# A two-layer hybrid encoder on one core: third buffers for split weights, splitting two places ahead in output projections, phases of a layer that overlap, and new row maxima and key sums in attention

## The chip, the cores and the metric

The kernel runs on one core of one Trainium2 chip. The metric is the device time of one execution in microseconds (us). Five engines work side by side, each through its own list of instructions in order: TensorE (PE, matrix products and transposes), VectorE (DVE), ScalarE (ACT), GpSimd (POOL) and SyncE (SP, which here issues every DMA). An instruction that waits for another engine holds up everything behind it on its own engine.

## The reference

Two layers are applied to x (1024 tokens by 1024 features, float32). Each layer projects x with one wide matrix, feeds the columns to four mixers, and projects the four outputs back:

```python
h = jnp.einsum('bsd,dn->bsn', x, w_in[i])
y_a = attention_branch(...)   # 8 query heads, 2 key heads, axial rotary positions
y_h = hgrn2_branch(...)       # gated linear recurrence, forward and backward
y_s = ssd_branch(...)         # Mamba-2 form with a depthwise conv, forward and backward
y_g = gla_branch(...)         # gated linear attention, forward and backward
out = jnp.einsum('bsn,nd->bsd', concatenate([y_a, y_h, y_s, y_g]), w_out[i])
x = layer_norm(DEEPNORM_ALPHA * x + out, ln_g[i], ln_b[i])
```

Attention is a softmax over 1024 keys of 64 elements for each of 8 heads, multiplied by the values and by a gate.

## The kernel before, in words

Matrix products against weights are made exact enough by splitting: a weight tile of 128x1024 arrives by DMA in two halves (`wraw`), ACT rounds it to the fast float format (`whi`) and POOL subtracts to get the rest (`wlo`). The activations are split in the same way (`xh`, `xl`; for the output projection `mxh`, `mxl`). Each product is three passes: whi with xh, whi with xl, wlo with xh. `w_load` issues the two loads, `w_conv` makes the splits, `w_get` takes the pair for a place (one weight tile of one item), and `w_ahead` splits the next place and loads the one after. There are three buffers for raw halves and two each for `whi` and `wlo`.

The program is written by a planner at build time. Work of two kinds is queued. *Fill* items (`F(...)`) are the projections, which are long runs of matrix products: input projections into 1024 columns of PSUM (`proj`) or 512 (`projh`), and output projections (`oproj`). *Lane* items (`M(...)`) are the mixers, generators that yield what they wait for. At every step `run` takes the lane item that the plan's clock says is ready first, or a piece of fill: fill comes when no lane is ready within a slack of 100 ns, or when `plan.behind(share)` says that PE has streamed fewer columns than `share` of a threshold in the present window of 3413 ns. `KNOBS` holds the slack and the share (0.5). An item opens when the items that it names are done. The finished order is static.

One layer runs through these stages. The half projections of attention's inputs come first. Attention then works tile by tile of 128 queries: `a_qprep` norms, rotates and splits the queries (`qr`, `qhl`, transposed to `QT`); `a_s` multiplies QT by the high part of the keys into 1024 columns of PSUM (`S`) and takes the row maximum on DVE (`mx`), four times for each of two key heads; `a_e` computes the transposed scores (`ST`, twice per block: with QT and with `QM`, which carries the maxima), ACT exponentiates into `Pt`, and POOL adds the eight `Pt` blocks of a tile (`psum`) to give the softmax sums; `a_pv` multiplies by the values (`O`, 64 output rows) and takes the sums across keys (`Z`). Then come four HGRN heads (`hp`, `hn`, `hm`), the SSD branch (`sB`, `sC`, `sx` convolutions on DVE, `sm`, `sw`), and GLA in two pairs of heads (`gp`, `gn`, `gm`). HGRN and GLA share a tree of seven levels (`tree`, products `lv` of 32 or 64 columns, each level waiting for DVE), state products (`kst`, `P`) and outputs (`ot`); GLA adds a norm (`gss`) for each output. HGRN runs its tree on all 128 rows of the PE array, GLA on two halves of 64 rows. While GLA runs, only the 32 places of a layer's output projection are left as fill. `spec_proj` and `spec_post` compute the gates of GLA (`gk`, `ga`, `gm`) and the decays of SSD. The layer norm ends the layer (`lnT`, in the second layer `outT`).

SBUF is shared out in slots: 62 of 2 KB per partition (`k2`), 8 of 4 KB (`k4`), and others. The planner waits for a slot where none is free. Large results go through DRAM (`hdr`, `yd`).

All engine calls pass through the planner's wrapper, so nearly every row of the profile has the line of its call, 299 (300 in the changed kernel). Names such as `lv` or `wlo` tell the rows apart.

## Time and profile before

| | |
|---|---|
| median of 3 runs | 2640.66 us (2638.04 to 2647.71) |
| profiled execution, its own time | 2644.85 us |
| span of the profiled execution, first to last instruction | 2643.0 us |
| outside the span | 1.85 us |
| PE busy | 2481.6 us (94%) |
| DVE busy | 1588.1 us (60%) |
| ACT busy | 1092.9 us (41%) |
| POOL busy | 1227.7 us (46%) |
| mean granted PE clock | 0.970 |
| moved by DMA | 284.38 MB, mean 108 GB/s |

Busy time is the time in which at least one instruction of an engine runs. The granted clock is the share of full speed that the chip gave to PE; in this trace it is 1 or one half at any moment. A matrix product of 512 columns is shown with a duration near 400 ns, but they are pipelined: what counts is the time from one start to the next. A float32 product shows as two rows for one instruction in the program, a product in the fast format as one.

### The profile page before, as it was taken

Reading aid. Unit: us, or ns where it says so; the run is one execution under the profiler, and the core shown is the slowest. Engines: PE = TensorE matmul, PEld = TensorE weight load, DVE = VectorE, ACT = ScalarE, POOL = GpSimd, SP = SyncE. Lnnn points to the kernel's source line nnn. Section 1 sums busy time; section 2 is a strip of 40 time slices with the busy share of each in tenths; the row PEclk is TensorE's granted clock in tenths of the full one; section 3 lists DMA queues with packets and bytes.
Section 4 is the critical chain, followed back from the end, with each engine's and each line's share of the span. In section 5 each row is a group of like instructions: output and inputs, shape, how many; then the busy total and the mean of one; then the engine's idle time right before and its main releaser. Section 6 shows DMA issues by size and latency. Waiting matters only on the chain. (4 is left out here: it accounts for less than half of the span.)

```text
span 2643.0 us, 46508 instructions
## 1 busy us (share of the span) xinstructions
PE 2481.6 (94%) x18352; PEld 1855.2 (70%) x18352; DVE 1588.1 (60%) x2895; ACT 1092.9 (41%) x2100; POOL 1227.7 (46%) x932
## 2 busy tenths in 40 slices
PE   8999899999989997889989999999999999988996
PEld 6855457777877886667777655577777787866675
DVE  2574520565489778863555745206664898868737
ACT  4445453332464433334344444533334543433342
POOL 3556663223335446423554566642223454564334
PEclk9999999999989998989999999999999899999998
DMA  6311112011137447622343111120111365676232
GB/s 210 100 48 52 36 43 66 33 53 49 46 112 252 148 148 256 218 71 89 100 162 112 64 38 48 51 68 29 57 41 46 131 237 152 189 262 203 79 104 100
DMA packets 170173, 284.38 MB, mean 108 GB/s; under 512 B 17780, under 2 KB 43380, under 8 KB 169956
## 3 DMA queue, kind: packets, MB, share of 16 engines
q1 hardware_dynamic: 169956, 281.41, 32.5%
q8 instruction: 145, 2.38, 0.4%
q14 instruction: 72, 0.59, 0.1%
HBM read 205.39 MB, written 75.96 MB: 106 GB/s over the span
## 5 line engine op out<-in xcount | busy, mean ns | idle before, releaser
L299 POOL TENSOR_TENSOR wlo<-wraw,whi 128x512 fp32r<-128x512 f32 x372 | 509.9, 1391 | 585.3 <-ACT whi L299 528.7
L299 PE MATMUL proj<-xh,whi 128*128 128x512 f32 x1056 | 429.4, 407 | 4.7 <-DVE u L299 4.7
L299 PE MATMUL proj<-xl,whi 128*128 128x512 f32 x1056 | 415.1, 393 | 0.0
L299 PE MATMUL projh<-xh,whi 128*128 128x512 f32 x704 | 287.8, 409 | 10.4 <-ACT whi L299 9.6
L299 POOL TENSOR_TENSOR psum<-psum,Pt 128x1024 f32<-128x1024 f32 x96 | 228.6, 2381 | 128.2 <-ACT Pt L299 123.1
L299 ACT CAST whi<-wraw 128x512 fp32r<-128x512 f32 x372 | 216.6, 623 | 165.0 <-DMA wraw<-in_wt 63.7
L299 PE MATMUL proj<-xh,wlo 128*128 128x512 f32 x1056 | 281.0, 400 | 0.0
L299 PE MATMUL projh<-xl,whi 128*128 128x512 f32 x704 | 280.2, 398 | 0.3 <-DVE xl L299 0.3
L299 PEld LDWEIGHTS proj<-xh,whi 128*128 128x128 f32 x1056 | 199.6, 189 | 49.1 <-ACT ga L299 5.5
L299 PE MATMUL oproj<-mxh,whi 128*128 128x512 f32 x512 | 217.8, 425 | 15.9 <-ACT whi L299 9.2
L299 PEld LDWEIGHTS proj<-xl,whi 128*128 128x128 f32 x1056 | 200.2, 190 | 37.2
L299 PEld LDWEIGHTS proj<-xh,wlo 128*128 128x128 f32 x1056 | 192.6, 188 | 41.3 <-issue 2.1
L299 ACT ACTIVATE Pt<-ST 128x512 f32<-128x512 f32 x256 | 151.1, 597 | 135.6 <-PE ST L299 133.8
L299 PE MATMUL oproj<-mxl,whi 128*128 128x512 f32 x512 | 206.2, 403 | 0.0
L299 PE MATMUL projh<-xh,wlo 128*128 128x512 f32 x704 | 193.9, 398 | 0.0
L299 DVE TENSOR_REDUCE mx<-S 128x1 f32<-128x1024 f32 x128 | 151.9, 1218 | 53.5 <-PE S L299 52.4
L299 DVE TENSOR_TENSOR QP<-QP,T 128x512 f32<-128x512 f32 x168 | 144.7, 861 | 48.4 <-PE lv L299 47.5
L299 PEld LDWEIGHTS projh<-xh,whi 128*128 128x128 f32 x704 | 134.8, 192 | 54.9 <-issue 13.4
L299 ACT COPY M<-C 128x256 f32<-128x256 f32 x168 | 69.4, 415 | 241.2 <-DVE C L299 241.2
L299 PE MATMUL oproj<-mxh,wlo 128*128 128x512 f32 x512 | 152.7, 412 | 4.1 <-POOL wlo L299 4.1
L299 PEld LDWEIGHTS projh<-xl,whi 128*128 128x128 f32 x704 | 134.9, 192 | 27.5 <-DVE xl L299 1.5
L299 PEld LDWEIGHTS projh<-xh,wlo 128*128 128x128 f32 x704 | 129.0, 189 | 35.3 <-issue 9.7
(241 smaller groups left out, 4602.1 us busy)
## 6 DMA issues: line engine op xcount, KB each, us to landing
wraw<-in_wt SPq DMA_DIRECT2D x244, 256.0 KB
wraw<-in_wo SPq DMA_DIRECT2D x128, 256.0 KB
hdr<-zs SPq DMA_DIRECT2D x64, 256.0 KB
zs<-hdr SPq DMA_DIRECT2D x64, 256.0 KB
bc<-dr SPq DMA_DIRECT2D x64, 256.0 KB
yld<-yd SPq DMA_DIRECT2D x56, 256.0 KB
hdr<-sp SPq DMA_DIRECT2D x40, 256.0 KB
yd<-o SPq DMA_DIRECT2D x40, 256.0 KB
```

What stands on the lines that cost most here:

```text
L299: return real(*args, **kw)
```

## The change

**Buffers.** `whi` and `wlo` get three buffers each; the 2 KB slots go from 62 to 58. `w_ahead` also splits the second next place, and loads the third, when the next place belongs to another item or to an output projection.

**The planner.** The share in `KNOBS` goes from 0.5 to 1.0, and the cost of a POOL instruction from 155 + 2.09 n to 160 + 2.17 n.

**Row maxima.** The queries are also rounded whole (`qp`, ACT), transposed (`qpT`, PE) and copied (`Q2`, ACT). `a_s` multiplies two heads at a time, one on rows 0 to 63 of the array and one on rows 64 to 127, with half of the keys each time; DVE takes two maxima per instruction and then one maximum of two halves. The queries' low part is no longer in these maxima, which are only the shift of the softmax.

**Key sums.** The adds of the `Pt` blocks move from POOL to DVE.

**Phase borders.** `spec_proj` and `spec_post` come at the start of a layer instead of after HGRN's projections. The first HGRN projection opens after attention tile 4 instead of 6, and the HGRN mixers no longer wait for the last attention tile. From attention tile 4 on, at most 4 instead of 7 or 8 of the blocks `Pt` are live. SSD's groups and GLA's loads open earlier (after HGRN head 2, after SSD mixer 2, and so on). `a_pv` gets a lane of its own. The products `CB` of SSD are released earlier.

```diff
-NK2 = 62
+NK2 = 58
+H0, NQ = 4, 4
-KNOBS = ((None, 100, 0.5),)
+KNOBS = ((None, 100, 1.0),)
...
-                cost = 155 + 2.09 * n + (120 if fn == "tensor_copy" else 0)
+                cost = 160 + 2.17 * n + (120 if fn == "tensor_copy" else 0)
...
-    NB = {"k2": NK2, "k4": NK4, "wraw": 3, "whi": 2, "wlo": 2, "st": 24, "t2": 2, "t4": 2, "t8": 2, "ts32": 2, "ts16": 2, "ts8": 2, "ts4": 6,
+    NB = {"k2": NK2, "k4": NK4, "wraw": 3, "whi": 3, "wlo": 3, "st": 24, "t2": 2, "t4": 2, "t8": 2, "ts32": 2, "ts16": 2, "ts8": 2, "ts4": 6,
...
                 w_load(nk)
+                if nk[0] is not fcur[0] or nk[0].name.startswith("o"):
+                    w_conv(nk)
+                    nk = w_key(2)
+                    if nk is not None:
+                        w_load(nk)
...
             def second_half():
                 ins = h_in.pop(h)
+                yield ["k4:2"]
...
-            yield [spec, w2]
+            yield [spec, w2, "k2:12"]
...
+                    qp = k2("qp", F32R)
+                    ac.copy(qp, qr)
+                    yield [qp, "A:1"]
+                    pt = transpose4(lambda c: qp[:, ck(c)], "qpT", F32R)
+                    Q2 = k2("Q2", F32R)
+                    ac.copy(Q2, pt.bitcast(F32))
...
-                for c in range(4):
-                    yield [QT, "P:1"]
-                    S = bigps("S")
+                for c in range(2):
                     for sh in range(2):
-                        mm(hs(S, sh), QT[:, ck(c)], KK[g * 2][sh], True, True)
-                    yield [S]
-                    ve.tensor_reduce(out=mx[:, c:c + 1], in_=S, axis=AX.X, op=ALU.max)
-                    drop(S)
+                        yield [Q2, "P:1"]
+                        S = bigps("S")
+                        for e in range(2):
+                            r = slice(e * 64, e * 64 + 64)
+                            mm(hs(S, e), Q2[r, ck(2 * g + c)], KK[g * 2][sh][r], True, True)
+                        yield [S]
+                        ve.tensor_reduce(out=mx[:, sh * 4 + 2 * c:sh * 4 + 2 * c + 2], in_=AV(S, 0, [[HALF, 2], [1, HALF]]), axis=AX.X, op=ALU.max)
+                        drop(S)
+                tt(ve, mx[:, 0:4], mx[:, 0:4], mx[:, 4:8], ALU.max)
...
-                    yield [lambda: live[0] < NP[li], "k4:1"]
+                    yield [lambda: live[0] < (NP[li] if ti < H0 else NQ), "k4:1"]
...
-                        tt(gp, acc_s, pts[ti, 0], P, ALU.add)
+                        tt(ve, acc_s, pts[ti, 0], P, ALU.add)
...
-                        tt(gp, acc_s, acc_s, P, ALU.add)
+                        tt(ve, acc_s, acc_s, P, ALU.add)
...
+        F(f"sp{li}", spec_proj, after=x1 + [f"set{li}"], ws=[wsrc("sp")])
+        M(f"spp{li}", spec_post, needs=[f"sp{li}"], lane=3)
-            M(f"aP{li}{ti}", a_pv(ti), needs=[f"akv{li}a", f"akv{li}b", f"az{li}3"])
+            M(f"aP{li}{ti}", a_pv(ti), needs=[f"akv{li}a", f"akv{li}b", f"az{li}3"], lane=11)
-            F(f"hp{li}{h}", h_proj(h), after=[f"hm{li}{h - 2}"] if h > 1 else [f"set{li}", f"aP{li}6" if h == 0 else f"aP{li}7"],
+            F(f"hp{li}{h}", h_proj(h), after=[f"hm{li}{h - 2}"] if h > 1 else [f"set{li}", f"aP{li}{H0}" if h == 0 else f"aP{li}7"],
-            M(f"hn{li}{h}", a, needs=[f"hp{li}{h}", f"aP{li}7"])
+            M(f"hn{li}{h}", a, needs=[f"hp{li}{h}"])
-        F(f"sp{li}", spec_proj, after=[f"hp{li}3"], ws=[wsrc("sp")])
-        M(f"spp{li}", spec_post, needs=[f"sp{li}", f"hm{li}2"], lane=3)
-            M(f"sgp{li}{g}", s_group_post(g), needs=[f"sB{li}{g}", f"sC{li}{g}"] + (exps if g == 0 else [f"sm{li}0"]), lane=3)
+            M(f"sgp{li}{g}", s_group_post(g), needs=[f"sB{li}{g}", f"sC{li}{g}"] + ([f"hm{li}2"] if g == 0 else [f"sw{li}1"]), lane=3)
-            M(f"gp{li}{p}", g_load(p), needs=names + ([f"sm{li}3"] if p == 0 else [f"gn{li}0"]), lane=8)
+            M(f"gp{li}{p}", g_load(p), needs=names + ([xlast, f"sm{li}2"] if p == 0 else [f"sm{li}3"]), lane=8)
```

How the order of instructions moves is shown at three places.

**VectorE in attention, first layer.** Before, the rows are the row maxima (`mx<-S`), what is made of them (`qhl`), a tile's result (`ya`) and a gate of the fill (`zs`):

```order
L299 TENSOR_REDUCE mx<-S 128x1 x4
L299 TENSOR_SCALAR qhl<-mx 128x4
L299 SCALAR_TENSOR_TENSOR qhl<-mx,qhl 128x4
L299 TENSOR_REDUCE mx<-S 128x1 x3
L299 TENSOR_TENSOR ya<-O,rz 128x512
L299 TENSOR_REDUCE mx<-S 128x1
```

In the changed kernel, the same engine and stage:

```order
L300 TENSOR_REDUCE mx<-S 128x2
L300 TENSOR_TENSOR psum<-psum,Pt 128x1024
L300 TENSOR_REDUCE mx<-S 128x2 x2
L300 TENSOR_TENSOR mx<-mx 128x4
L300 TENSOR_SCALAR qhl<-mx 128x4
L300 SCALAR_TENSOR_TENSOR qhl<-mx,qhl 128x4
L300 TENSOR_TENSOR psum<-psum,Pt 128x1024
```

The adds of `Pt` now stand between the maxima; POOL's list, which had 112 of them, has none left.

**TensorE in GLA, first layer, second pair of heads.** `lv ... 64x64` are the last two levels of the tree, `oproj` is the fill. Before:

```order
L299 MATMUL lv<-QP,M 64x64 x16
L299 MATMUL oproj<-mxh,whi 128x512
L299 MATMUL oproj<-mxl,whi 128x512
L299 MATMUL lv<-QP,M 64x64 x16
L299 MATMUL oproj<-mxh,whi 128x512
```

In the changed kernel:

```order
L300 MATMUL lv<-QP,M 64x64 x16
L300 MATMUL oproj<-mxh,whi 128x512
L300 MATMUL oproj<-mxl,whi 128x512
L300 MATMUL oproj<-mxh,whi 128x512
L300 MATMUL oproj<-mxl,whi 128x512
L300 MATMUL oproj<-mxh,whi 128x512
L300 MATMUL oproj<-mxl,whi 128x512
L300 MATMUL oproj<-mxh,wlo 128x512 x4
L300 MATMUL oproj<-mxh,whi 128x512
L300 MATMUL oproj<-mxl,whi 128x512
L300 MATMUL lv<-QP,M 64x64 x16
```

Between these two levels stood 2 products of fill, and now 12. Counted over the order from GLA's first `lv` to its last `gss`, a layer has 324 output-projection products inside GLA in the first layer and 392 in the second before, 502 and 472 after; behind it stand 358 and 242 before, 202 and 176 after.

**SyncE at the first output projection, first layer.** `yld` are the mixer results that it reads, `wraw<-in_wo` its weights, `M`, `q` and `T` GLA's inputs. Before:

```order
L299 DMA hdr<-u 128x512
L299 DMA yld<-yd 128x512 x4
L299 DMA wraw<-in_wo 128x512 x4
L299 DMA xr<-in_xT 128x512
L299 DMA hdr<-zs 128x512 x2
```

In the changed kernel:

```order
L300 DMA yld<-yd 128x512 x4
L300 DMA M<-hdr 128x512
L300 DMA q<-hdr 128x512
L300 DMA T_9150<-hdr 128x512 x2
L300 DMA wraw<-in_wo 128x512 x4
L300 DMA hdr<-zs 128x512
```

Four loads of GLA now stand between the results and the first output weights.

More of the change, by code (lines that the diff above doesn't have):

```diff
@@ L1265, in gen @@
                     yield None
-                sd["g", g] = (Cc, CB, Bt)
+                sd["g", g] = (Cc, Bt)
+                sd["cb", g] = CB
             return gen
@@ L1290, in gen @@
                 colA, dr = sd["colA"], sd["dr"]
-                CB = sd["g", n // 2][1]
+                CB = sd["cb", n // 2] if n % 2 == 0 else sd.pop(("cb", n // 2))
                 def rows(hf, e):
@@ L1592, in gen @@
                         ac.copy(QT, pt.bitcast(F32))
-                        qts[ti, g] = (QT, qhl)
+                        qts[ti, g] = (QT, Q2, qhl)
             return gen
@@ L1600, in gen @@
                 yield [lambda: (ti, g) in qts]
-                QT, qhl = qts.pop((ti, g))
-                mx = mt("c8", [128, 4], name="mx")
-                for c in range(4):
-                    yield [QT, "P:1"]
-                    S = bigps("S")
-                    for sh in range(2):
-                        mm(hs(S, sh), QT[:, ck(c)], KK[g * 2][sh], True, True)
-                    yield [S]
-                    ve.tensor_reduce(out=mx[:, c:c + 1], in_=S, axis=AX.X, op=ALU.max)
-                    drop(S)
+                QT, Q2, qhl = qts.pop((ti, g))
+                mx = mt("c8", [128, 8], name="mx")
+                for c in range(2):
+                    for sh in range(2):
+                        yield [Q2, "P:1"]
[6 more added lines that the diff above has]
+                        drop(S)
+                del Q2
+                tt(ve, mx[:, 0:4], mx[:, 0:4], mx[:, 4:8], ALU.max)
+                mx = mx[:, 0:4]
                 mh = AV(qhl, 64, [[128, 4]])
```

4 lines of the change are left out of this document (2 added, 2 removed).

## The prediction, written before the changed kernel ran

> **What bounds the kernel now.** I read the page's first part, then PE's time by stages, PE's waits, and single groups and instructions.
>
> The page's first part:
>
> ```profile
> PE 2481.6 (94%) x18352; PEld 1855.2 (70%) x18352; DVE 1588.1 (60%) x2895; ACT 1092.9 (41%) x2100; POOL 1227.7 (46%) x932
> ```
>
> PE is the bound over the whole program, with 2643.0 - 2481.6 = 161 us in which it does nothing. To that comes time at half clock: a mean clock of 0.970 is a loss of 0.03 x 2643 = 79 us if PE had work all that time. So at most some 240 us can be won without taking work off PE. The windows by stage tell where they lie. The columns are the stretch, then its length, and for PE, PEld, DVE, ACT and POOL the busy time, then granted clock, DMA share and GB/s:
>
> ```profile
> 154.00:396.00 242.00, 222.36 (x927) 126.42 (x928) 117.86 (x131) 121.32 (x201) 150.91 (x77) 0.98 0.13 41
> 396.00:726.00 330.00, 327.39 (x3045) 253.37 (x3042) 147.25 (x316) 115.95 (x232) 104.02 (x91) 1.00 0.15 50
> 726.00:770.00 44.00, 37.34 (x298) 27.46 (x297) 37.04 (x52) 30.67 (x48) 20.21 (x18) 0.84 0.27 97
> 990.00:1041.00 51.00, 37.17 (x193) 30.55 (x192) 40.12 (x76) 18.12 (x36) 32.59 (x26) 0.87 0.81 254
> 1041.00:1197.00 156.00, 135.12 (x2263) 99.06 (x2261) 117.40 (x229) 53.37 (x103) 66.16 (x66) 0.88 0.45 150
> 1320.00:1408.00 88.00, 76.86 (x335) 61.69 (x334) 46.37 (x82) 39.82 (x71) 47.95 (x38) 0.94 0.49 164
> 1496.00:1628.00 132.00, 122.90 (x517) 71.73 (x517) 70.95 (x87) 67.25 (x112) 81.60 (x43) 0.96 0.15 48
> 2046.00:2068.00 22.00, 17.46 (x171) 10.46 (x169) 20.71 (x31) 15.62 (x24) 6.49 (x5) 0.73 0.29 108
> 2310.00:2360.00 50.00, 43.20 (x212) 33.88 (x210) 33.34 (x52) 17.91 (x32) 35.66 (x28) 0.93 0.78 251
> 2360.00:2553.00 193.00, 174.49 (x2508) 129.16 (x2508) 133.35 (x258) 68.85 (x130) 76.91 (x77) 0.96 0.44 147
> 2618.00:2643.00 25.00, 1.96 (x14) 1.35 (x12) 18.59 (x34) 3.84 (x14) 7.45 (x5) 0.59 0.30 115
> ```
>
> I call a stage's *loss* its idle PE time plus (1 - clock) times its length. HGRN's stretch (396 to 726) loses 3 us: there nothing is to be won. GLA loses 20.9 + 18.7 = 39.6 us in the first layer (1041 to 1197) and 18.5 + 7.7 = 26.2 in the second (2360 to 2553). The end of HGRN, where the gates are computed, loses 13.7 and 10.5 (726 to 770, 2046 to 2068). The entry to the output projections loses 20.4 and 10.3, with the DMA engines at 0.81 and 0.78. Attention loses 24.4 and 14.4. The layer border (1320 to 1408) and the last 25 us are not touched by the change. PE's waits name what ends them:
>
> ```profile
> PE lv L299 <- DVE QP L299: 12.8, 26, 1.6
> PE projh L299 <- ACT whi L299: 9.6, 4, 5.5
> PE oproj L299 <- ACT whi L299: 9.2, 1, 9.2
> PE gk L299 <- DVE near L299: 4.8, 2, 3.0
> PE proj L299 <- DVE u L299: 4.7, 2, 2.8
> PE oproj L299 <- POOL wlo L299: 4.1, 5, 2.3
> ```
>
> No single wait is large: the loss is many short ones (us in total, times, longest), and the half clock after them.
>
> **The change, part by part.** *Products of the row maxima.* The old pair of S, the start of a group of four transposes, and two stretches of `ot`, which HGRN does on all 128 rows and GLA in turn on 128 (AT) and 64 rows (QP). First the S pair (start, duration):
>
> ```profile
> 200.26 0.46 PE L299 MATMUL qmT<-ident,qhl 128*128 128x128 f32 x4
> 200.55 0.69 PE L299 MATMUL projh<-xh,wlo 128*128 128x512 f32 x2
> ...
> 204.75 0.62 PE L299 MATMUL S<-KK,QT 128*128 128x512 f32 x2
> 205.20 0.39 PE L299 MATMUL ST<-QT,KK 128*128 128x512 f32 x1
> 205.43 0.39 PE L299 MATMUL ST<-QM,KK 128*128 128x512 f32 x1
> ```
>
> Then HGRN's `ot`, and GLA's:
>
> ```profile
> 1989.51 0.39 PE L299 MATMUL ot<-AT,V 128*128 128x128 f32 x2
> 1989.73 0.61 PE L299 MATMUL ot<-QP,S 128*128 128x128 f32 x4
> 1990.18 0.39 PE L299 MATMUL ot<-AT,V 128*128 128x128 f32 x2
> ```
>
> ```profile
> 2449.30 0.49 PE L299 MATMUL ot<-AT,V 128*128 128x128 f32 x2
> 2449.72 0.71 PE L299 MATMUL ot<-QP,S 64*128 64x128 f32 x4
> 2450.36 0.49 PE L299 MATMUL ot<-AT,V 128*128 128x128 f32 x2
> ```
>
> A pair of S takes 205.20 - 204.75 = 0.45 us, a product 0.23. The same six `ot` take 0.67 us in HGRN and 1.06 in GLA: going to half the rows and back costs 0.39 us. The change has 128 pairs of S on half the rows, in the order almost always between products on all rows. If the halves run at once, a pair takes 0.23 + 0.39 = 0.62, or 0.17 more than now: +22 us. If they run one after the other, 0.84: +50. If the halves run at once and the turn costs nothing, -0.22 each: -28. I take +22, since the turn is in the trace. The new transposes are 16 groups of four at 0.29: +5. Together +27 us of PE work in a stage that is bound by PE.
>
> The Trainium skill speaks for the other end: TensorEngine Tiling (Array Packing), section Theoretical Speedup, gives up to twice the speed where the contraction is 64 or less, and the sum by that alone would be the -28 for this part. Its section Key Properties says that changing the tiling mode drains the engine; the 0.39 us agrees with that.
>
> *Key sums.* The rows for what moves, and for what VectorE takes for such operands:
>
> ```profile
> L299 POOL TENSOR_TENSOR psum<-psum,Pt 128x1024 f32<-128x1024 f32 x96 | 228.6, 2381 | 128.2 <-ACT Pt L299 123.1 <-PE S L299 4.4
> L299 POOL TENSOR_TENSOR psum<-Pt 128x1024 f32<-128x1024 f32 x16 | 38.0, 2377 | 23.5 <-ACT Pt L299 23.5
> L299 DVE TENSOR_TENSOR QP<-q,T 128x1024 f32<-128x1024 f32 x24 | 34.6, 1443 | 7.5 <-DMA T<-hdr 7.5
> L299 DVE TENSOR_TENSOR QP<-QP,T 128x512 f32<-128x512 f32 x168 | 144.7, 861 | 48.4 <-PE lv L299 47.5
> L299 DVE TENSOR_TENSOR acc<-acc,oproj 128x512 f32<-128x512 f32 x96 | 62.5, 680 | 64.3 <-PE oproj L299 63.7
> ```
>
> POOL is rid of 267 us. DVE has no such add now: twice 680 to twice 861 ns are the ends, 1.36 to 1.72 us, and the 1443 of a row with the same size and two operands in SBUF is nearest. 56 adds a layer are 81 us. DVE's load in two equal stretches of attention:
>
> ```profile
> 132.00:396.00 264.00, 244.36 (x1024) 140.18 (x1024) 135.44 (x152) 129.53 (x216) 162.51 (x82) 0.98 0.14 44
> 1452.00:1716.00 264.00, 253.67 (x1101) 155.13 (x1102) 137.30 (x165) 132.39 (x224) 167.42 (x85) 0.98 0.15 48
> ```
>
> 137 + 81 = 218 of 264 us, or 83%. PE's fill hides it while DVE keeps up, so I cost it at nothing; that cover is the first rival below. The other additions (two ACT copies per tile, a maximum of 4 columns on DVE) go the same way; ACT stands at half there (130 of 264).
>
> *Attention's losses*, 24.4 + 14.4 = 39 us: what is won is bounded by 0 and 39. POOL's splits no longer queue behind 2.38 us adds, and HGRN's projections come in as fill; DVE gets slower to answer. I take 11.
>
> *Fill beside GLA.* The order puts 178 more output products beside GLA in the first layer and 80 in the second; at 0.23 us these are 41 and 18 us of work that now stands alone. They can hide at most the stage's loss, 39.6 and 26.2, and at most their own length: so the ends are 0 and 39.6 + 18 = 58. I take about 70%, 28 and 12, because the order is fixed in advance and some gaps fall elsewhere.
>
> *Gates early.* `gk` and its chain leave the end of HGRN, where the losses are 13.7 + 10.5 = 24 us. The convolutions (`u`), which DVE does there, stay. Ends 0 and 24; I take 14, since the wait of `gk` (4.8) is as long as that for `u` (4.7) and the half clock follows both. In attention, where they go, the gates find a PE that has fill.
>
> *Third buffers and two places ahead.* They can take the waits for `wlo` (4.1) and part of those for `whi` in `projh` (9.6, of which one of 5.5): ends 0 and 14, I take 5. The wait of 9.2 us for the first output weights stays, since raw halves still have three buffers and the first item's loads come late. In the changed order four more loads of 128x512 float32 stand before them on SyncE: 4 x 0.262 MB at the 254 GB/s of that stage are 4 us later. What queues behind them is the first `whi`, and PE behind that. Net 1 us won. The four slots fewer are made up by `CB` being released early; if not, loads of GLA wait, inside the bounds above.
>
> *The sum.* Won: 28 + 12 + 14 + 1 + 11 = 66. Added: 27. Net -39 on the profiled execution's 2644.85 us: 2605.9. That execution is 4.2 us above the median of 2640.66, so the forecast is 2601.7, written as 2602 us.
>
> **The rivals.** *VectorE becomes the bound of attention.* Adds stand between the maxima that PE waits for, and S has only two buffers. With the gates' VectorE work, which I put at some 6 us a layer from this row, DVE has 224 of 264 us to do:
>
> ```profile
> L299 DVE TENSOR_SCALAR gm<-gk,pk 128x512 f32<-128x512 f32 x16 | 11.6, 748 | 6.2 <-ACT ga L299 5.9
> ```
>
> It decides once DVE's remaining idle is over 264 - 224 = 40 us a stage. It idles 127 now; if half of that stays, the stage needs 288: 24 us more a layer, 48 in all, and the 11 us are not won. 2602 + 48 + 11 = 2661, slower than before. For it speaks DVE's 83%; against it, that attention gets more fill, which PE can do while DVE is late. Chance 0.16.
>
> *GLA is bound by its own chain.* Each of its levels waits for DVE (`lv` on `QP`), and DVE is busy 117 of 156 us. Then more fill beside it makes the stage longer by as much as is taken off behind it, but for half: 20 of the 40 are not won, and attention wins nothing (11). 2602 + 31 = 2633, no change. That the splits two places ahead do little, as raw halves remain three, is included. Chance 0.17.
>
> *The halves of S run at once and turn for free.* Then the part gives -28 instead of +22: 2602 - 50 = 2552. Against it stands the 0.39 us of `ot`; for it, that `ot`'s halves depend on each other's sums and those of S do not. Chance 0.12. This is what the Trainium skill's speedup of up to two (TensorEngine Tiling, Theoretical Speedup) would give.
>
> **How the numbers follow.** The forecast has 0.55, with its own range of 2575 to 2627 from the ends of its terms taken a third of the way. The range reaches from just below the third rival to the first: 2545 to 2661. About 0.5%, 13 us, is what a measurement of this kernel can tell from no change: faster means below 2627.5, slower above 2653.9. Faster: 0.52 of the forecast, 0.12, and 0.07 of the second rival: 0.71. Slower: 0.14 of the first rival and 0.01 of the second: 0.15. The rest, 0.14, is the same.
>
> **What would show it.** In the changed profile, S should appear with 64 rows, and the time from the start of a pair to the next product should be near 0.6 us; 0.25 or less would prove the third rival. GLA's two stretches should have a clock near 1 and losses of some 12 and 14 us in place of 39.6 and 26.2. `gk` should lie inside attention, and the end of HGRN lose some 5 us each time. DVE should be busy 80 to 90% in attention with PE still over 92%; PE below that, waiting for `qhl` or for S's buffers, would prove the first rival. PE's busy time should rise, not fall, by about what S adds, and its idle time drop by some 40 us. The prediction is wrong if attention plus HGRN take longer than before by more than 30 us, or if GLA's stretches lose as much as now.

## The result, and the profile after

The changed kernel takes 2705.49 us (median of 4 runs, 2700.67 to 2707.48), the kernel before 2641.24 us beside it: a ratio of 1.0237, with a 95% interval of 1.0213 to 1.0262. It is some 63 us slower, where 39 us less were forecast, and it lies outside the range. Ratios compare fast executions alone: one execution of the run with the maxima alone took 5380.06 us at a clock of 0.459, and its ratio leaves that one out. The profiled execution took 2700.67 us, with a span of 2698.9 us against 2643.0: 55.9 us more.

TensorE's busy time on the first part of the page after, beside the other engines:

```profile
PE 2506.7 (93%) x18416; PEld 1837.8 (68%) x18416; DVE 1676.4 (62%) x3039; ACT 1111.9 (41%) x2134; POOL 955.4 (35%) x820
```

TensorE is idle for 2698.9 - 2506.7 = 192 us instead of 161, and its mean clock is 0.968 instead of 0.970. In the prediction's count (idle + (1 - clock) x length) the loss is 279 us instead of 240, 39 more; by this count the other 17 us of the 56 are work. The forecast had a loss 66 us smaller and 27 us more work.

Where the loss lies is read from windows by stage. The borders are events, so that they fit both kernels: attention from its first key transpose to its last `Z`, the middle (HGRN, SSD) from there to the first `oproj`, the output stage (the end of SSD, GLA, output products) from there to the first `lnT`, or to the last product in the second layer. Before, first and then second layer:

```profile
57.00:415.00 358.00, 334.89 (x1447) 206.80 (x1447) 177.09 (x261) 168.35 (x321) 210.41 (x123) 0.99 0.18 58
415.00:1008.00 593.00, 569.86 (x4500) 459.20 (x4496) 381.25 (x745) 236.48 (x455) 220.55 (x186) 0.98 0.33 107
1008.00:1277.00 269.00, 243.16 (x2779) 184.84 (x2780) 169.06 (x308) 95.63 (x177) 125.61 (x112) 0.92 0.45 149
...
1390.00:1739.00 349.00, 335.99 (x1481) 215.24 (x1483) 170.21 (x263) 170.81 (x325) 213.93 (x125) 0.99 0.19 62
1739.00:2315.00 576.00, 564.39 (x4477) 453.69 (x4474) 391.10 (x757) 232.84 (x449) 219.31 (x187) 0.99 0.33 108
2315.00:2620.00 305.00, 279.35 (x2999) 212.44 (x2999) 200.68 (x372) 114.18 (x250) 144.90 (x127) 0.96 0.46 151
```

The same stages of the changed kernel:

```profile
57.00:466.00 409.00, 393.19 (x1697) 239.63 (x1699) 229.05 (x335) 189.61 (x360) 97.61 (x79) 0.98 0.18 59
466.00:1010.00 544.00, 518.98 (x4262) 417.37 (x4262) 351.48 (x722) 224.67 (x428) 191.66 (x171) 0.98 0.34 110
1010.00:1290.00 280.00, 239.73 (x2806) 182.25 (x2806) 180.38 (x327) 97.63 (x184) 133.80 (x117) 0.93 0.45 145
...
1400.00:1812.00 412.00, 383.54 (x1662) 226.09 (x1662) 253.04 (x368) 219.33 (x402) 102.97 (x85) 0.99 0.20 64
1812.00:2338.00 526.00, 520.00 (x4248) 420.05 (x4249) 326.02 (x651) 185.08 (x371) 179.99 (x161) 1.00 0.32 102
2338.00:2676.00 338.00, 302.71 (x3083) 232.30 (x3082) 239.49 (x445) 121.75 (x267) 158.68 (x137) 0.91 0.46 148
```

Each row's length less PE's busy time, plus half of its time at half clock (taken from the trace's clock record, finer than the two decimals shown), gives the losses:

| loss in us | before | after | forecast of the change | measured |
|---|---|---|---|---|
| attention, both layers | 28.2 + 18.1 | 22.6 + 31.9 | -11 | +8 |
| middle, both layers | 35.0 + 18.4 | 35.2 + 7.7 | -14 | -11 |
| output stage, both layers | 48.1 + 37.6 | 59.1 + 66.0 | -41 (28 + 12 + 1) | +39 |
| layer border | 14.9 | 16.9 | 0 | +2 |

The output stages lose where they should have won, and this is 80 of the 95 us by which the forecast was wrong. TensorE's waits name what ends them (us in total, times, longest):

```profile
PE oproj L300 <- DVE acc L300: 30.2, 11, 7.5
PE projh L300 <- ACT whi L300: 17.9, 6, 5.7
PE oproj L300 <- ACT whi L300: 14.2, 2, 9.7
...
PE qpT L300 <- ACT Pt L300: 8.6, 4, 4.1
```

Output products wait 30.2 us for `acc`, 5.3 before. That is VectorE adding `xr` to a product's result, and it frees the PSUM buffer for the next product. Why it comes late stands in SyncE's own list (start, duration) at the first output products of the changed kernel:

```profile
1019.67 8.41 SPq L300 DMA_DIRECT2D wraw<-in_wo  x4
...
1028.61 0.42 SPq L300 DMA_DIRECT2D xr<-in_xT  x1
```

Four raw halves are issued in a row against three buffers. SyncE stands 8.41 us in them, and the load of `xr` that VectorE needs is behind.

In the second layer the last products of GLA are alone. The windows of that stretch (the columns as before):

```profile
2576.80:2587.00 10.20, 8.17 (x44) 6.07 (x45) 3.08 (x10) 1.70 (x4) 2.58 (x8) 0.50 0.33 96
2587.00:2597.00 10.00, 8.61 (x25) 5.71 (x25) 0.46 (x1) 2.62 (x4) 0.00 (x0) 0.50 0.03 10
2597.00:2607.00 10.00, 7.72 (x22) 4.99 (x22) 0.57 (x2) 2.94 (x5) 1.27 (x1) 0.50 0.00 0
2607.00:2614.00 7.00, 6.79 (x30) 5.34 (x30) 4.88 (x8) 2.33 (x5) 1.27 (x1) 0.50 0.00 0
```

For 44.4 us from 2576.8 on the clock is one half, which costs 22 us of work at full speed.

Finally, SSD now runs beside GLA: its last run of products `yo` begins 51 us (first layer) and 54 us (second) after GLA's first `lv`, where it began 11 and 20 us ahead of it before. "SSD's end" below means this start. The first layer, before and then after (start, duration):

```profile
1030.63 1.83 PE L299 MATMUL yo<-u,S 128*128 128x128 f32 x14
...
1041.51 0.76 PE L299 MATMUL lv<-q,ks 64*32 64x32 f32 x64
```

```profile
1040.00 0.76 PE L300 MATMUL lv<-q,ks 64*32 64x32 f32 x64
...
1090.93 1.83 PE L300 MATMUL yo<-u,S 128*128 128x128 f32 x14
```

### The profile page after: what moved, and what is told of

Its sections match the earlier page's. It is cut to its first block, busy times and chain, and to the rows that moved or that the text cites. A ratio compares the mean times of both kernels' runs of the same rounds, so it can differ in the third digit from the quotient of the medians.

```text
span 2698.9 us, 46777 instructions
## 1 busy us (share of the span) xinstructions
PE 2506.7 (93%) x18416; PEld 1837.8 (68%) x18416; DVE 1676.4 (62%) x3039; ACT 1111.9 (41%) x2134; POOL 955.4 (35%) x820
## 5 line engine op out<-in xcount | busy, mean ns | idle before, releaser
L300 PE MATMUL projh<-xh,whi 128*128 128x512 f32 x704 | 293.2, 416 | 21.4 <-ACT whi L300 17.9
L300 PE MATMUL oproj<-mxh,whi 128*128 128x512 f32 x512 | 220.9, 432 | 45.6 <-DVE acc L300 30.2
L300 PEld LDWEIGHTS proj<-xh,whi 128*128 128x128 f32 x1056 | 199.0, 188 | 55.9 <-issue 7.9
L300 PEld LDWEIGHTS proj<-xh,wlo 128*128 128x128 f32 x1056 | 193.7, 189 | 41.5 <-issue 1.7
L300 DVE TENSOR_TENSOR QP<-QP,T 128x512 f32<-128x512 f32 x168 | 157.6, 938 | 43.3 <-PE lv L300 42.4
L300 DVE TENSOR_TENSOR psum<-psum,Pt 128x1024 f32<-128x1024 f32 x96 | 121.1, 1262 | 100.5 <-ACT Pt L300 99.9
L300 DVE TENSOR_REDUCE mx<-S 128x2 f32<-128x1024 f32 x128 | 154.2, 1219 | 36.1 <-PE S L300 35.9
L300 PEld LDWEIGHTS oproj<-mxh,whi 128*128 128x128 f32 x512 | 100.8, 197 | 74.7 <-ACT whi L300 18.2
```

The source lines that it names most:

```text
L300: return real(*args, **kw)
```

## The experiments

Ratios are to runs of the kernel before on the same chip, with 95% intervals; 0.01 is 26 us. The expectations count a stage's loss a little differently: its length less its products at the median time from one start to the next in the first two traces. That gives larger numbers (67 and 77 for the output stages after) in the same order. My theory at the outset had three costs: SyncE's stops, fill spent too early beside GLA, and S on half rows; the rivals stand in each expectation. The runs are grouped by question, not by time. The planner lays out everything that follows an edit anew, so four runs were built to keep the order of the changed kernel, or of another run, on the engines that compute.

### SyncE's stops: the third load later, all else in the same order

The second argument makes `w_load` hold its two loads back until the next weight is asked for, behind `xr`. Only SyncE's list differs from the changed kernel's. Of the edit, the call:

```diff
-                        w_load(nk)
+                        w_load(nk, nk[0].name.startswith("o"))
```

> The changed kernel with the same order on TensorE, VectorE, ScalarE and GpSimd. Only on SyncE the two loads of the third place's raw halves, where they are for an output projection, stand later: behind the next load of xr, or before the next weight is taken. Nothing is left out. My theory: these loads wait for raw buffers and hold up xr behind them, so SyncE's stops of 7 to 8 us shrink to about half, TensorE's wait of output products for acc falls from 30 us to some 15, and the time by 10 to 20 us: about 2690 us. Rival: SyncE is held up by the second place's loads already, or acc waits for VectorE's own queue: the same time within 5 us. Rival two: the weights come later and TensorE waits for whi instead: slower by 5 to 10 us.

Measured: 2689.99 us, ratio 1.0210 (1.0182 to 1.0237); the span is 11.8 us shorter than after. SyncE at the same place, and TensorE's wait:

```profile
1020.19 1.04 SPq L300 DMA_DIRECT2D wraw<-in_wo  x2
1021.42 0.33 SPq L300 DMA_DIRECT2D hdr<-u  x1
1022.11 0.33 SPq L300 DMA_DIRECT2D xr<-in_xT  x1
...
1023.50 5.43 SPq L322 DMA_DIRECT2D wraw<-in_wo  x2
```

```profile
PE oproj L300 <- DVE acc L300: 16.6, 6, 5.8
PE oproj L300 <- ACT whi L300: 14.7, 2, 10.3
```

`xr` is issued 6.5 us earlier, the wait for `acc` falls from 30.2 to 16.6, and that for `whi` does not grow. The two output stages lose 16 us less (59.1 + 66.0 to 55.2 + 53.9). The stops are a cause. Their size is less sure here: 12 us by the spans, 15.5 by the medians, and 7 by the ratios, whose intervals overlap (1.0213 to 1.0262 for the changed kernel).

### One place ahead again

```diff
-                if nk[0] is not fcur[0] or nk[0].name.startswith("o"):
-                    w_conv(nk)
-                    nk = w_key(2)
-                    if nk is not None:
-                        w_load(nk)
```

> The changed kernel with the five lines taken out that split two places ahead; third buffers for split weights stay, and nothing of the computation is left out. The planner orders the rest anew, so some 10 us of scatter are to be allowed for. My theory: with three raw halves, splitting two places ahead makes SyncE wait inside the weight loads, and the loads of xr behind them come late; VectorE's adds of xr and then TensorE wait. Then TensorE's wait of output products for acc goes from 30 us to below 10, SyncE's long weight loads (7 to 8 us) go, and the time is 15 to 30 us shorter: about 2680 us. Rival: the splits two places ahead are what the third buffers are for, and without them TensorE waits for whi and wlo: the waits for whi grow by what those for acc lose, the time stays at 2700 to 2710 us or grows.

Measured: 2689.52 us, 1.0191 (1.0174 to 1.0208). The time is as I expected, but the wait for `acc` fell only to 17.8 us, and the waits for `whi` of output products grew from 14.2 to 16.9: part of each theory. The loss fell by 20 us in the second layer's output stage (66.0 to 45.5), but rose by 4 in the first layer's, and it fell by 14 in the first layer's attention (22.6 to 8.5), where no output products are; so this run shows a new order as much as its edit.

### GLA after SSD

```diff
-            M(f"gp{li}{p}", g_load(p), needs=names + ([xlast, f"sm{li}2"] if p == 0 else [f"sm{li}3"]), lane=8)
+            M(f"gp{li}{p}", g_load(p), needs=names + ([f"sm{li}3"] if p == 0 else [f"gn{li}0"]), lane=8)
```

> The changed kernel with GLA's loads opening as before (first pair of heads after SSD's last mixer, second pair after the first has begun); nothing is left out, and the planner orders what follows anew. In the kernel before with the borders alone, GLA ran beside SSD for 13 us in the first layer, where the output stage lost 6 us less than before, and for 51 us in the second, where it lost 28 us more. Theory: two chains of mixers beside each other wait on VectorE and GpSimd and use up the fill, so without the overlap the two output stages lose 60 + 55 us instead of 67 + 77, and the time is 15 to 30 us shorter: about 2683 us. Rival: the overlap is harmless, and what costs in these stages is SyncE's stops in the weight loads alone: 2700 to 2710 us.

Measured: 2663.76 us, 1.0102 (1.0081 to 1.0123): 36 us less than the changed kernel by the ratios, more than I expected. SSD's end is 14 and 16 us ahead of GLA's first level. The output stages:

```profile
1008.00:1276.00 268.00, 238.20 (x2790) 180.63 (x2791) 175.47 (x325) 95.80 (x179) 130.37 (x115) 0.95 0.48 153
2323.00:2639.00 316.00, 284.49 (x2996) 217.30 (x2994) 211.57 (x379) 115.93 (x251) 146.50 (x127) 0.94 0.46 150
```

They lose 44.2 + 52.0 us instead of 59.1 + 66.0, and the whole loss of the run (232 us) is a little under that of before (240). But 12 us of what this run won lie in the second layer's attention (31.9 to 19.7), where no GLA runs: part of the gain is the new order.

### GLA after SSD, and the third load later

The two edits together; on the engines that compute, the order is that of the run above.

> The changed kernel with GLA's loads opening as before, and on SyncE the third place's weight loads behind the next load of xr; on the other engines the order is that of the run with GLA's loads alone (2663.8 us). Nothing is left out. Theory: SyncE's stops are a cost of their own, and the late load takes 10 to 15 us here too: about 2650 us, with TensorE's wait of output products for acc below 5 us instead of 10. Rival: with GLA's loads out of the way SyncE's stops cost little, and the run stays at 2660 to 2667 us.

Measured: 2642.45 us, 1.0007 (0.9992 to 1.0022). With these two edits the whole slowdown is gone. The run loses 212 us, 28 less than before, and by the same count has 25 us more work; the maxima alone bring 20 of that (below). The output stages:

```profile
1008.00:1265.00 257.00, 237.91 (x2790) 180.82 (x2790) 177.58 (x325) 94.64 (x178) 130.88 (x114) 0.93 0.49 160
2312.00:2618.00 306.00, 279.84 (x2998) 213.97 (x2997) 209.60 (x381) 111.26 (x243) 148.49 (x127) 0.95 0.46 153
```

They lose 36.8 + 41.5 us, 18 less than with GLA's edit alone. GLA's edit wins 31 us of these two stages with the third load late (109.1 to 78.3) and 29 without it; both pairs compare the same two orders. The way was not the one I gave. TensorE's waits with GLA's edit alone, and then with both:

```profile
PE P L300 <- ACT KST L300: 10.6, 5, 7.7
PE oproj L300 <- DVE acc L300: 10.2, 2, 5.1
...
PE yd L300 <- POOL Wm L300: 5.9, 2, 4.6
PE oproj L300 <- POOL wlo L300: 4.6, 1, 4.6
```

```profile
PE oproj L300 <- DVE acc L300: 14.2, 2, 7.5
...
PE P L300 <- ACT KST L300: 2.5, 3, 1.6
...
PE yd L300 <- POOL Wm L300: 1.2, 1, 1.2
```

The wait for `acc` grew. What fell are waits for ScalarE and GpSimd: those for `KST` and `Wm`, steps of the mixers, and the one for `wlo`, a weight split, which is gone. That the loads on SyncE are the cause is shown, since nothing else differs; by which load each step was held up is not.

### Less fill early beside the second layer's GLA

```diff
-KNOBS = ((None, 100, 1.0),)
+KNOBS = (("gp10", 100, 1.0), (None, 100, 0.3))
```

> The changed kernel, but from the moment that the second layer's GLA has its first inputs the planner's share is 0.3 instead of 1.0. Nothing is left out, and the order of all engines up to there is the same. Inside GLA stand 442 output products instead of 472, and they are spread otherwise: 240 instead of 338 before the first output of the first pair of heads, 144 + 8 + 32 + 8 instead of 82 + 0 + 6 + 10 in the second pair. My theory: the share of 1.0 spends the fill in the first pair and leaves the second pair bare, where the clock falls to one half for 44 us. Then this kernel has no such stretch, and the second layer's tail ends some 20 to 30 us earlier: about 2680 us. Rival: GLA's length there is set by its own chain of levels and the fill's place does not matter: 2700 to 2710 us, with the half clock as long as before or only moved. Rival two: products that are not spent early come behind GLA, and nothing is won in sum: the same time, with a clock near 1.

Measured: 2705.44 us, 1.0251 (1.0230 to 1.0272): no gain. The stretch of 44 us at half clock is gone, but others of 13.7 and 23.9 us stand earlier, and the stage loses 64.4 us instead of 66.0. My theory of the fill falls; the first rival holds: where the same products stand beside GLA only moves the half clock.

### The share alone, and the cost figure alone

Both start from the kernel before and change one number.

```diff
-KNOBS = ((None, 100, 0.5),)
+KNOBS = ((None, 100, 1.0),)
```

> The kernel before with the planner's share at 1.0 instead of 0.5 and nothing else; nothing is left out. Inside GLA stand 386 and 408 output products instead of 324 and 392. Theory after the run with later fill: where the fill stands beside GLA does not move the time, so this is within 10 us of before: 2630 to 2650 us. The prediction: fill beside GLA hides in the stage's gaps, 62 + 16 products of 0.23 us, 70% of them: 13 us less, 2626 us. Rival: a share of 1.0 pushes fill ahead of mixer steps that are ready and VectorE's chain comes late for it: 2650 to 2670 us.

Measured: 2646.29 us, 1.0034 (1.0020 to 1.0048). The output stages lose 52.6 + 47.1 instead of 48.1 + 37.6, though 62 and 16 more products stand beside GLA; the first layer's middle loses 15.0 instead of 35.0. In sum the share is nearly neutral.

```diff
-                cost = 155 + 2.09 * n + (120 if fn == "tensor_copy" else 0)
+                cost = 160 + 2.17 * n + (120 if fn == "tensor_copy" else 0)
```

> The kernel before with one number changed: the planner's cost of a GpSimd instruction, 160 + 2.17 n instead of 155 + 2.09 n, as in the change. Same instructions, same engines, nothing left out; only the order that the planner finds is another. Theory: the old order was a good one of many, and any new order of the same work costs 10 to 30 us, mostly in the output stages: 2650 to 2670 us. Rival: the order scatters to both sides by a few us: 2632 to 2645 us, and then what the single parts of the change cost is theirs.

Measured: 2669.57 us, 1.0117 (1.0096 to 1.0137). The same instructions on the same engines, ordered by a figure that is 4% larger, take 31 us more. The first layer's output stage holds 19 of them (67.5 us against 48.1). There 182 output products stand ahead of GLA's first level (86 before), and 14 instead of 186 are left between GLA's end and the first `lnT`; GLA's last four outputs have 10 products between them, where they had 46. So a new order alone can cost some 30 us, and nothing shows that this is the most: single effects of such a size from runs with a new order are not safe by themselves.

### Third buffers, two places ahead and 58 slots alone

The kernel before with these three hunks of the change.

> The kernel before with third buffers for whi and wlo, splitting two places ahead, and 58 slots of 2 KB; nothing is left out. Theory: splitting two places ahead with three raw halves makes SyncE stop in weight loads, with the loads of xr behind them; from the changed kernel it took 15 us when undone, so here it adds about 15: 2650 to 2660 us, with TensorE's wait of output products for acc well over the 5 us of before. Rival: it hurts only where GLA's early loads stand on SyncE too, and so alone it is neutral or wins the waits for wlo: 2630 to 2645 us.

Measured: 2715.23 us, 1.0282 (1.0259 to 1.0305), slower than the whole change and than either theory. The wait for `acc` is 19.8 us, as my theory had it, but the most is in the first layer's output stage, which loses 97.6 us. In its order 328 output products stand ahead of GLA, and 24 between its end and the first `lnT`. Whether the four missing slots hold GLA back there was not tried.

### The phase borders alone, and the gates alone

The kernel before with all border hunks; then with only the two lines that move `spec_proj` and `spec_post` to the start of a layer, and the `k2:12` wait.

> The kernel before with the phase borders of the change alone: gates at the start of a layer, HGRN's projections from attention tile 4, at most four live blocks Pt from there, SSD's groups and GLA's loads earlier, the early release of CB, a lane of its own for a_pv. Share 0.5, old buffers, old maxima, key sums on GpSimd; nothing is left out. Theory: GLA now begins while SSD still runs (in the changed kernel the last product of SSD comes 51 and 54 us after GLA's first level, before it came 11 and 20 us ahead of it). VectorE then serves two chains at once, and TensorE waits for both; this is what the second layer's GLA loses more, 24 us. Then this kernel is 15 to 30 us slower than before: 2655 to 2670 us. Rival, the prediction: gates inside attention win 14 us at the end of HGRN and the overlap costs nothing: about 2625 us. The planner orders all anew, with some 10 us of scatter.

Measured: 2670.50 us, 1.0115 (1.0095 to 1.0135), as the theory had it. The middle loses 13.6 + 8.4 instead of 35.0 + 18.4 us: 31 won, more than the 14 that I gave the gates. The first layer, with SSD ending 13 us into GLA, has an output stage that loses 42.5 us (48.1 before); the second, with 51 us, loses 68.9 (37.6 before). Attention loses 35.8 in the second layer, 18 more.

> The kernel before with one part of the change: the gates of GLA and SSD are computed at the start of a layer; nothing else is changed or left out. Theory: this is the part that won. With all borders the stretch from attention's end to the first output product lost 31 and 27 us instead of 44 and 33, which is 19 us, and the prediction put the gates at 14. So about 2622 us, faster than both kernels. Rival: the gates' steps in attention make TensorE wait there (the second layer's attention lost 25 us more with all borders), and the planner's new order eats the gain: 2635 to 2650 us.

Measured: 2703.27 us, 1.0246 (1.0219 to 1.0272), against both theories. The middle does win, 19.4 + 14.1 instead of 35.0 + 18.4, but the output stages lose 79.7 + 59.5: the order has 226 and 242 products ahead of GLA. What the gates win (20 us), the output stages lose nearly threefold (54). That the new order alone does this is likely, but not shown.

### S on all rows, in the same order

The edit, shortened: the planner is still given the old operands, so that the order stays.

```diff
-   mm(hs(S, e), Q2[r, ck(2 * g + c)], KK[g * 2][sh][r], True, True)
+   mm(hs(S, e), QT[:, ck(2 * c + e)], KK[g * 2][sh], True, True)
```

> The changed kernel with the same instructions in the same order on all engines, but each product of the row maxima takes the old operand on 128 rows of the array (the queries' high and low part, QT) instead of Q2 on 64 rows. The maxima then hold the low part again; all else is as in the changed kernel, so the new transposes and copies of Q2 are still made and not used. Theory of the prediction: going to half the rows and back costs 0.39 us and the halves run at once, so 128 pairs are 0.17 us cheaper here: 22 us less, about 2683 us. What the two traces already show (S itself 10 us cheaper, the products behind it some 20 us dearer) makes it 10 to 13 us: about 2693 us. Rival: the halves at once are worth more than the turn; then this kernel is slower than the changed one, 2710 us or more. If S waits for QT, which comes later than Q2, that shows as waits of TensorE for QT, to be taken off.

Measured: 2709.28 us, 1.0274 (1.0253 to 1.0295): the gain of work did not reach the time, for S waits 15.1 us for `QT`, which the order makes later than `Q2`, and more half clock follows (108 us lost to it instead of 87). The price itself can be read. The same place on half rows (changed kernel) and on all rows (start, duration):

```profile
135.04 0.49 PE L300 MATMUL S<-KK,Q 64*128 64x512 f32 x2
135.47 0.51 PE L300 MATMUL ST<-QT,KK 128*128 128x512 f32 x1
135.81 0.40 PE L300 MATMUL ST<-QM,KK 128*128 128x512 f32 x1
...
136.28 0.40 PE L300 MATMUL projh<-xl,whi 128*128 128x512 f32 x1
136.61 0.49 PE L300 MATMUL S<-KK,Q 64*128 64x512 f32 x2
```

```profile
135.06 0.62 PE L300 MATMUL S<-KK,QT 128*128 128x512 f32 x2
135.51 0.39 PE L300 MATMUL ST<-QT,KK 128*128 128x512 f32 x1
135.74 0.39 PE L300 MATMUL ST<-QM,KK 128*128 128x512 f32 x1
...
136.19 0.39 PE L300 MATMUL projh<-xl,whi 128*128 128x512 f32 x1
136.42 0.62 PE L300 MATMUL S<-KK,QT 128*128 128x512 f32 x2
```

From one start to the next, the pair takes 0.43 us against 0.45, the product behind it 0.34 against 0.23, and the product ahead of the next pair 0.33 against 0.23. Over both attention stretches at full clock, idle time left out, a product of S takes 0.216 us against 0.253, but `projh` 0.246 against 0.238 and `ST` 0.287 against 0.273: in sum 770.0 against 758.5 us. Half rows cost 11.5 us of work; the turn is paid by the neighbours.

### Key sums on GpSimd, in the same order; sums and maxima alone

```diff
-                        tt(ve, acc_s, acc_s, P, ALU.add)
+                        tt(gpv, acc_s, acc_s, P, ALU.add)
```

`gpv` issues on GpSimd, and the planner counts it as VectorE's, so that the order stays.

> The changed kernel in the same order of work, with the 112 adds of the key sums issued on GpSimd again instead of VectorE; no other engine's order changes, and nothing is left out. Theory: VectorE at 65% of the second layer's attention holds up nothing by these adds alone, and GpSimd at 20% has room, so the time stays within 8 us of the changed kernel's 2705. Rival, the first rival of the prediction in a smaller form: the adds stand between maxima, gates and queries on VectorE and make TensorE wait for qpT, S and ST; then taking them off wins 15 us or more, most of it in the second layer's attention, which loses 54 us against 25 before. Rival two: GpSimd is slower (2.4 us an add) and Z waits for it: 10 us slower.

Measured: 2718.38 us, 1.0322 (1.0296 to 1.0348): slower than the changed kernel, near rival two's 10 us. But `Z` waits for the sums only 2.5 us in all, so the wait that rival two named is not what costs; the waits of `qmT` for VectorE's `qhl` grew from 1.5 to 6.9 us, and the rest of the way stays open. The adds on VectorE, and on GpSimd in this run:

```profile
L300 DVE TENSOR_TENSOR psum<-psum,Pt 128x1024 f32<-128x1024 f32 x96 | 121.1, 1262 | 100.5 <-ACT Pt L300 99.9
```

```profile
L300 POOL TENSOR_TENSOR psum<-psum,Pt 128x1024 f32<-128x1024 f32 x96 | 229.6, 2391 | 126.8 <-ACT Pt L300 123.3 <-PE qpT L300 2.3
```

Moving the sums helps: the second layer's attention loses 44.8 us with them on GpSimd and 31.9 without. VectorE is not the bound there (253 of 412 us).

From the kernel before, with the sums alone, then the maxima alone, then both (the hunks of the change):

> The kernel before with the key sums on VectorE and nothing else; nothing is left out. Theory: in the order of the changed kernel the adds cost 13 us less on VectorE than on GpSimd, since splits and Z do not wait behind 2.4 us adds; here GpSimd is fuller (46%), so 5 to 15 us are won: about 2630 us, faster than both kernels. Rival: the second layer's attention, which loses 25 us before, loses 15 to 25 more, and the time is 2650 to 2660 us.

> The kernel before with the new row maxima and nothing else; nothing is left out but the queries' low part in the maxima. Theory: products on half rows cost nothing net, but qpT adds 6 us of work and a step that waits for ScalarE (9 us of waits for Pt and qp in the second layer's attention of the changed kernel), so 15 to 25 us more: 2655 to 2665 us, most of it in attention. Rival: the maxima cost only their 6 us and the sums on VectorE make the rest: 2640 to 2648 us.

> The kernel before with the new row maxima (Q2, half rows) and the key sums on VectorE, and no other part of the change; nothing is left out but the queries' low part in the maxima, as in the change. Theory: the products on half rows cost nothing net (S 13.5 us cheaper and ST and projh 13.6 us dearer in the same order), the transposes 6 us, and the second layer's attention loses 28 us more because ScalarE and VectorE have more to do between the steps of a tile: about 2665 us, with TensorE's waits for Pt in the second layer's attention. Rival: attention's loss comes from the borders (four live blocks Pt, HGRN's fill) and not from here: 2640 to 2650 us. The prediction's own sum for this part was +27 - 11: 2657 us.

Measured: sums 2643.46 us, 1.0013 (1.0000 to 1.0027); maxima 2660.07, 1.0075 (1.0053 to 1.0096); both 2684.25, 1.0165 (1.0141 to 1.0188). With the sums alone attention loses 27 us instead of 46, and the new order gives this back in the middle (+3) and the output stages (+17). With the maxima alone the losses in sum are as before (236 us against 240) and the time is 20 us longer: by the prediction's count that is work. The time is what I expected, but the way is not: I gave it 6 us of work and the rest to waits in attention. Both together are worse than their sum by more than the intervals, and I have no reason for it but the order.

### Eight live blocks in the second layer

```diff
-                    yield [lambda: live[0] < (NP[li] if ti < H0 else NQ), "k4:1"]
+                    yield [lambda: live[0] < (NP[li] if ti < H0 or li else NQ), "k4:1"]
```

> The changed kernel with the limit of four live blocks Pt from attention tile 4 on kept in the first layer only; in the second layer eight may live, as before. Up to there the order is the same on all engines, and nothing is left out. Theory: with four blocks ScalarE's exponentials and the products by the values go in lockstep, and TensorE waits for Pt (qpT and ST together 14 us in the second layer's attention); with eight these waits fall below 5 us and the second layer's attention loses some 35 us instead of 54: about 2687 us. Rival: the waits come from the order of ScalarE's list (copies of Q2 and qhl between the exponentials), not from the limit: 2700 to 2710 us.

Measured: 2691.58 us, 1.0201 (1.0176 to 1.0226). The theory falls: `qpT` and `ST` wait nearly as long as in the changed kernel (7.2 and 7.0 us, 8.6 and 6.9 there), and the second layer's attention loses 41.6 instead of 31.9. The gain lies in its output stage (42.1 instead of 66.0), where SSD now ends 11 us into GLA and not 54.

### The parts that won, together

The changed kernel with GLA after SSD, the third load later, the old maxima, and the old share; in the first of two also the old GpSimd cost.

> The changed kernel with GLA's loads opening as before, the third place's weight loads behind xr, the old row maxima, and the planner's share and GpSimd cost as before. Nothing is left out. Theory: with both cures the changed kernel came to 2642; the new maxima alone cost 19 us in the kernel before, so without them some 15 to 20 us less: about 2625 us, faster than both kernels. Rival: the planner's new order takes this back, as it did in the run with the cost figure alone (29 us): 2640 us or more.

> As the run before (GLA's loads as before, late third load, old row maxima, share as before), but with GpSimd's cost in the planner as in the change. Nothing is left out. Theory: about 2625 us as well, within the scatter of the planner's order, which I put at 10 us where few output products stand ahead of GLA (here 48 and 126). Rival: the order scatters by up to 30 us even so: then the two runs lie far apart.

Measured: 2622.74 us, 0.9948 (0.9928 to 0.9968), faster than both kernels by its interval; and 2642.41 us, 1.0016 (0.9998 to 1.0033). The first one's output stages:

```profile
1001.00:1245.00 244.00, 226.94 (x2728) 171.94 (x2727) 162.85 (x284) 93.90 (x172) 122.43 (x107) 0.96 0.50 162
2312.00:2595.00 283.00, 268.24 (x2967) 206.85 (x2965) 198.99 (x352) 111.48 (x241) 145.70 (x122) 0.98 0.47 158
```

They lose 26.9 + 19.4 us, the least of all. The second run differs in one planner number and loses 37.3 + 44.8: the rival's scatter of some 18 us is real even between two good orders.

### All output stages side by side

The 40 output stages of the 20 kernels, by their order:

| output stage | stages | mean loss | from, to |
|---|---|---|---|
| SSD ends 40 us or more after GLA's first level | 14 | 60 | 45.5, 68.9 |
| not so, and 180 or more output products ahead of GLA | 5 | 71 | 52.6, 97.6 |
| neither | 21 | 42 | 19.4, 56.3 |

In the third group 314 to 522 products stand inside GLA, and the loss does not follow that number: 48.1 us with 324, 41.0 with 438, 52.0 with 460, 42.1 with 522. The ranges of the groups overlap, and the 14 stages of the first group come from only 6 orders, since several runs share one. So this is a pattern and no proof; of the four runs in one order none moves GLA's start.

## Why the prediction was wrong

- **Fill beside GLA (28 + 12 us won).** This step failed. The order did put 178 and 80 more products inside GLA, but more fill did not use up the stage's gaps. The run with later fill and the share alone show no gain from the products' place or number, and the table shows none. The two stages lost 39 us more, entry included.
- **What took its place.** I costed the borders by the gates alone and never GLA's earlier start, though the hunk was in the diff. GLA beside SSD is probably the larger cost: undoing it gave 36 us. But the loss fell by 29 us in the output stages and by 12 in an attention where no GLA runs, and the cost figure alone shows that a new order can make 31.
- **Third buffers and two places ahead (net 1 us won).** I saw that raw halves still had three buffers, and that loads queue on SyncE, but priced only four loads of GLA at 4 us of transfer. The step missed SyncE waiting inside the weight loads, 8.41 us in one place, with everything behind it. Undone in one order, this is 7 to 15.5 us in the changed kernel and 21 to 25 after GLA's edit.
- **Gates early (14).** Near in size by luck: the middle lost 11 us less, all of it in the second layer, where `gk` runs at 1453 to 1482 us, inside attention. In the first layer `gk` runs at 472 to 496 us, behind attention's last `Z` (467), and the middle loses 35.2 us as before. With the borders alone it lies at 110 to 138 us there, and that middle loses 13.6. Why the changed order puts it late is open. The gates alone, in the order then made, were 65 us slower.
- **Attention's losses (11 won).** Wrong in sign: 8 lost, 14 more in the second layer and 6 less in the first. Part of this is `qpT`, a new step that waits for ScalarE (8.6 us for `Pt`). The live blocks are not the cause; the rest stays open.
- **S on half rows (+22) and `qpT` (+5).** The mechanism holds: in the quoted place a pair and its two neighbours' delays come to 0.43 + 0.11 + 0.10 = 0.64 us, where the forecast had 0.62 for halves at once with a turn, 0.84 for halves in turn, and 0.23 for a free turn. Over the stage it is 11.5 us and not 22, mostly because a pair on all rows also takes 0.5 us there, not the 0.45 that I read at one place. The Trainium skill (TensorEngine Tiling (Array Packing), Theoretical Speedup) has up to twice the speed for a contraction of 64; between products on all rows nothing of it was left here.
- **Key sums (nothing).** They were worth 13 us by the medians and 22 by the ratios, in the same order. The rival that VectorE becomes the bound gave the right sign for the whole (2661 us) by the wrong cause: VectorE is busy 61% of the second attention, and an add takes 1.26 us there, not the 1.44 of the forecast.
- **The second rival** (GLA bound by its own chain) came nearest in mechanism: with the share alone, more fill beside GLA won nothing, and the two output stages lost 14 us more. It stopped at no gain, since I did not price SSD's chain beside it.

What stays open: the 36 us of GLA's start were only seen with a new order, so that this cause is argued and not shown, while SyncE's stops are shown; and the scatter of orders is not explained, only measured.

## What to carry to other kernels

Before counting gaps as room for more fill, ask which chains share an engine in that stage and what a queue in order (here SyncE) has standing behind a wait; a prefetch one deeper than its buffers turned the queue itself into the wait (8.41 us in one place). Where a planner orders the work, move one number that should not matter first: here it made 31 us, and only runs that keep the order settle smaller causes.

## What the runs showed of the hardware that was not expected

TensorE's clock stayed at one half for 44.4 us although its instructions filled 6.79 of 7.00 us in the last of the windows quoted (2607 to 2614); what ran in the whole stretch, up to the `oproj` below, were `kst`, `P`, `ot` and `gss`. The Trainium skill (TensorE: Matmul & The Clock Gate, What's actually happening) has the full clock come back after about 3.4 us of a busy engine. This trace does not agree: from 2607.2 to 2621.1 the profile, in which the ends of products are modelled, shows TensorE without a gap, and the clock is one half. So being busy in the profile is not enough here; full clock came back at 2621.2, 5.4 us after this first `oproj`, which streams 512 columns on all rows. What counts stays open:

```profile
2615.76 0.79 PE L300 MATMUL oproj<-mxh,whi 128*128 128x512 f32 x1
```

In attention here a change of rows is paid in the product ahead of it and the one behind, not in the product on half rows: 0.33 and 0.34 us instead of 0.23, while the pair itself looks cheaper, 0.43 instead of 0.45 us.
